# One polynomial moved from GpSimd to VectorE, and a changed start, last group and ending of a mixture-of-experts stage (hybrid decoder trunk, one core)

## The chip, the cores and the metric

The kernel runs on one core of a Trainium2 chip. The metric is the time of one execution on the device in microseconds, as the median of several executions. TensorE (PE in the rows) does the matrix products; PEld is its loading of stationary operands. VectorE is DVE, ScalarE is ACT, GpSimd is POOL, and SP is the engine whose queue issues most transfers.

## What is computed

The input is 1024 tokens of width 1024. The trunk has one layer, so only the Mamba-2 mixer runs, then the expert mixture, the per-layer embedding and a final norm:

```python
h = x
h = h + ssd_mixer(rms_norm(h, ssd_norm), ...)      # dt = softplus(dt_raw + dt_bias), used by the scan
h = h + hier_moe(rms_norm(h, moe_norm), ...)       # 8 groups x 8 experts, top-1 group, top-2 experts in it
gate = sigmoid(rms_norm(h, ple_norm) @ ple_w_gate + ple_b_gate)
h = h + gate * (p @ ple_w_proj)
return rms_norm(h, final_norm)
```

Each of the 64 experts is silu(x @ w_gate) * (x @ w_up) @ w_down with 1024 x 512 weights, so the expert weights are 402.7 MB in fp32 and every one is read once.

## The kernel before

**Mixer (`ssd`).** The tokens are worked in two halves of 512. In each half the input projection runs through four groups of ten column tiles, every product as three fp32r matmuls (high x high, low x high, high x low, L220 to L222), which need each weight split on ScalarE and VectorE (`split`, L70 and L71). Beside it the scan of the group before runs in pieces that a small plan places. `step_sizes` (L225) computes softplus: exp on ScalarE, then s = e/(e+2), q = s*s, and an eight-term polynomial in q by Horner's rule. VectorE computes the first term (L258); seven rounds of a product and a sum are done on GpSimd (L260, L261); VectorE multiplies the result by s (L262). `norm` (L436) makes the row norms of a scan unit on VectorE through `rsqrt` (lines 57 to 67, tiles `nt` and `rs`), and `store` (L444) transposes them on TensorE (L447).

**Order.** Where the text below says that TensorE's order is written by hand, `manual_schedule` fixes it. The order on the other engines is made by a planner ahead of time, from program order and from estimated times. On the chip each engine then takes its instructions in that order.

**Loading of experts.** The unit is a slab of 1 MB ([128, 2048] fp32). `moe_weights.loads` (L840) is a generator that is stepped once per step of the output projection: the gate weights `wpg` of the embedding, the norms, and then the first nine slabs, seven into the ring's buffers (`RING = 7`) and two into `self.spare`, the pair buffers in which later tokens of the groups are gathered. `moe` then loads three more into `ring2`, `yx` and `vx` (L1009). From there `half` (L861) loads each slab into the next of eight buffers, seven of `ring` and one of `ring2`; the load waits in SP's queue until TensorE is through with the buffer's old slab.

**Groups.** For each of the eight groups, `steps` is a list of pieces of the expert products: `up` (gate and up products of two experts side by side, two pieces each) and `down`. One piece is 16 records of L1098 on two slabs. `fill` puts other work behind a numbered step, in TensorE's hand-written order. From the second group on it holds the embedding of the group before (`ple`, L939): statistics and transposes (L972, `tr`), eight `gate` pieces of two fp32 matmuls each (L980; each is two records), and two `add` pieces. Before the last group there are two such sets, for the group's rows and for the overflow rows; each has 12 pieces, at the steps listed in L1334. `wk`, `ps1`, `ps2` are small pools; `sts`, `S` hold selection matrices. `fetch_p` (L926) gathers the projected embedding rows into `p0` and `po` on GpSimd's queue.

**Ending.** The last group's last two down products and its own embedding are done together by `ending` (L1179) in four column quarters q. `product(q)` is the down product (slabs from `columns`), `turn(q)` combines the quarter into the rows and transposes it, `gate(q, j)` is the gate product in three fp32r passes (`parts`, L932), and `halves(q)` splits the gate weights of the quarter into high and low parts, on ScalarE (L1239) and GpSimd (L1240), into one buffer that all quarters use in turn. `add(j)` (L1250) applies the sigmoid, multiplies, adds, squares, and lets GpSimd multiply by the final norm's weights (L1262). Two engines then scale by the norm, and GpSimd's queue issues the indirect store (L1281). `combine(3, 1)` (L1283, L1204) finishes the overflow rows.

Of the kernel before, what the change touches and what calls it, by code (L numbers as in the profile page):

```python
# [42 lines left out]
class K:  # L43
# [64 lines left out]
    def ssd(self, left, right):  # L108
# [116 lines left out]
        def step_sizes(hf):  # L225
# [604 lines left out]
    def moe_weights(self, st):  # L830
# [9 lines left out]
        def loads():  # L840
# [12 lines left out]
            self.first = first = [(s_, k0, e + b) for e, s_ in ((0, wg), (0, wu), (2, wg)) for k0 in (0, 4) for b in range(2)]  # L853
            for i, (src, k0, e) in enumerate(first[:RING + 2]):
                w = self.spare[i - RING].rearrange("p i d -> p (i d)") if i >= RING else None
                self.ready.append(self.half(src, e, k0, 4, w))
                yield

        return loads()

    def half(self, src, e, k0, n, w=None):  # L861
# [3 lines left out]
        if w is None:  # L865
            self.turn = (self.turn + 1) % (RING + 1)
            w = (self.ring2 if self.done and self.turn == 0 else self.ring).tile([128, 2048], F32, name="w")
# [4 lines left out]
    def columns(self, src, e, cs):  # L872

        self.turn = (self.turn + 1) % (RING + 1)
        w = (self.ring if self.turn else self.ring2).tile([128, 2048], F32, name="w")
# [5 lines left out]
    def moe_buffers(self, st, ring):  # L881
# [4 lines left out]
        self.p0, self.po = (hp.tile([128, D], F32, name=f"p{i}") for i in range(2))  # L886
        self.iall = hp.tile([128, NGR + NSET], I32, name="iall")
        for x in (self.h0[0], self.ho[0], self.p0, self.po):
            nc.gpsimd.memset(x, 0.0)
# [49 lines left out]
    def ple(self, h, pr, store, wk, pq_, pc_, own=()):  # L939
# [27 lines left out]
        def tr(k0):  # L967
            if k0 == 0:
# [4 lines left out]
            nc.scalar.activation(V["vT"][:, k0:k0 + 4], pt, AF.Copy)  # L973

        def gate(hf, k0):
# [3 lines left out]
            for k in (k0, k0 + 1):  # L979
                nc.tensor.matmul(V["pq"], lhsT=V["vT"][:, k], rhs=wpg[:, k, cs], start=(k == 0), stop=(k == KD - 1))  # L980
# [19 lines left out]
    def moe(self, s2, ring, sa):  # L1000
# [8 lines left out]
        for n, w in enumerate((self.ring2.tile([128, 2048], F32, name="w"), y0, vx)):  # L1009
            src, k0, e = self.first[RING + 2 + n]  # L1010
            self.ready.append(self.half(src, e, k0, 4, w))
# [161 lines left out]
        def ple_of(G, i, own=part):  # L1173
# [3 lines left out]
                bounds_check=T - 1, oob_is_err=False), wk, ps1, ps2, own)  # L1177

        def ending(G):  # L1179
# [52 lines left out]
            def halves(q):  # L1232
                if q == 0:
                    B["w"] = gp.tile([128, 2, 2, 2, 512], F32R, name="XT")
# [285 lines left out]
```

## Time and profile before

| what | value |
|---|---|
| median of 3 executions | 1903.54 us (1902.07 to 1907.86) |
| the profiled execution's own time | 1900.96 us |
| its span in the profile | 1899.0 us |
| TensorE busy | 1823.4 us, 96% |
| VectorE, ScalarE, GpSimd busy | 1032.4, 754.1 and 192.6 us |
| moved by DMA | 548.23 MB |

The span runs from the first to the last record of the execution; 2 us of its time lie outside it. In rows of instructions the first number is the start or the busy time, as each group says; a bracket at the end gives the idle time of the engine just before, and what ended it.

### The profile page before, as it was taken

What the parts mean: (1) busy time and instruction counts of PE and PEld (TensorE: products, weight loads), DVE (VectorE), ACT (ScalarE), POOL (GpSimd) and SP (SyncE); (2) the same over time, 40 slices, a digit from 0 to 9 for tenths busy, and PEclk for the clock granted to TensorE, in tenths of its full rate; (3) what the DMA queues carried; (4) which work ended last, traced back from release to release, by engine and by line L of the source; (5) the groups of instructions that cost most, each with busy time, mean ns of one, the idle gap of its engine ahead of it and who ended that gap; (6) DMA issues with size and microseconds to landing.
All of it is one profiled execution on the core that took longest, in us unless ns stands there. A gap on an engine that the chain in (4) does not pass through costs nothing. (4 is left out here: it accounts for less than half of the span.)

```text
span 1899.0 us, 23199 instructions
## 1 busy us (share of the span) xinstructions
PE 1823.4 (96%) x8692; PEld 1039.2 (55%) x8692; DVE 1032.4 (54%) x2195; ACT 754.1 (40%) x1044; POOL 192.6 (10%) x276
## 2 busy tenths in 40 slices
PE   6999999999999999999999999999999999999996
PEld 3877877778787778873443343433433334334334
DVE  4588889868988866574341433423415243243223
ACT  5577767567776533332121222211212222122223
POOL 0210122202210131012000000000000000000014
PEclk9999999999999999999999999999999999999998
DMA  9343545345334686958999999999999999999993
GB/s 312 97 115 102 141 114 142 92 121 136 107 87 114 209 320 208 349 190 332 423 421 417 404 421 406 418 421 400 422 413 408 421 411 417 421 402 421 344 346 103
DMA packets 195543, 548.23 MB, mean 289 GB/s; under 512 B 16480, under 2 KB 129376, under 8 KB 147296
## 3 DMA queue, kind: packets, MB, share of 16 engines
q1 hardware_dynamic: 179296, 519.32, 73.1%
q10 hardware_dynamic: 11872, 14.51, 2.2%
q0 software_dynamic: 4256, 12.85, 1.8%
q8 instruction: 70, 1.15, 0.3%
q14 instruction: 49, 0.40, 0.1%
HBM read 527.37 MB, written 21.89 MB: 289 GB/s over the span
## 5 line engine op out<-in xcount | busy, mean ns | idle before, releaser
L220 PE MATMUL mm<-xh,wh 128*128 128x512 f32 x640 | 264.7, 414 | 1.3 <-ACT wh L70 1.3
L222 PE MATMUL mm<-xh,wl 128*128 128x512 f32 x640 | 252.4, 394 | 4.1 <-DVE wl L71 4.1
L221 PE MATMUL mm<-xl,wh 128*128 128x512 f32 x640 | 251.2, 393 | 0.0
L1098 PE MATMUL pup<-w,XT 128*64 128x512 f32 x1016 | 243.6, 598 | 3.6 <-DMA w<-in_w_up_dram 3.6
L1098 PE MATMUL pgate<-w,XT 128*64 128x512 f32 x1000 | 231.8, 598 | 0.0
L1098 PE MATMUL py<-w,hT 128*64 128x512 f32 (+1 forms) x1024 | 226.0, 584 | 2.1 <-DMA w<-in_w_down_dram 2.1
L71 DVE TENSOR_TENSOR yx<-py,yx 128x512 fp32r<-128x512 f32 (+1 forms) x68 | 44.8, 659 | 215.7 <-ACT yx L70 215.7
L1098 PEld LDWEIGHTS pup<-w,XT 128*64 128x64 f32 x1016 | 77.8, 136 | 139.6 <-issue 120.3
L1098 PEld LDWEIGHTS py<-w,hT 128*64 128x64 f32 x1024 | 70.8, 136 | 143.7 <-issue 134.4
L1098 PEld LDWEIGHTS pgate<-w,XT 128*64 128x64 f32 x1000 | 68.5, 136 | 134.0 <-issue 131.5
L222 PEld LDWEIGHTS mm<-xh,wl 128*128 128x128 f32 x640 | 120.8, 189 | 32.9 <-DVE wl L71 7.0
L220 PEld LDWEIGHTS mm<-xh,wh 128*128 128x128 f32 x640 | 121.1, 189 | 31.5 <-issue 4.6
L221 PEld LDWEIGHTS mm<-xl,wh 128*128 128x128 f32 x640 | 121.4, 190 | 29.4 <-issue 5.7
L980 PE MATMUL pq<-wpg,vx 128*128 128x512 f32 x256 | 123.2, 607 | 0.0
L71 DVE TENSOR_TENSOR wl<-w,wh 128x1024 fp32r<-128x1024 f32 x80 | 97.9, 1223 | 39.6 <-ACT wh L70 39.5
L1129 ACT ACTIVATE hT<-pt 128x512 f32<-128x512 f32 x31 | 18.4, 595 | 241.0 <-PE pt L1127 241.0
L70 ACT ACTIVATE wh<-w 128x1024 fp32r<-128x1024 f32 x80 | 84.3, 1053 | 74.1 <-PE mm L221 62.7
L333 DVE SCALAR_TENSOR_TENSOR xbc<-raw,convw,xbc 128x512 f32<-128x512 f32 x144 | 107.5, 749 | 3.2 <-ACT xbc L331 2.4
L70 ACT ACTIVATE yx<-py 128x512 fp32r<-128x512 f32 (+1 forms) x68 | 38.9, 572 | 159.4 <-PE py L1098 159.4
L567 PE MATMUL mm<-wl,yh 128*128 128x512 f32 x256 | 98.7, 395 | 2.4 <-DVE wl L578 2.4
L568 PE MATMUL mm<-wh,yl 128*128 128x512 f32 x256 | 97.3, 392 | 0.0
L566 PE MATMUL mm<-wh,yh 128*128 128x512 f32 x256 | 96.2, 401 | 0.7 <-ACT yh L70 0.7
(354 smaller groups left out, 2789.7 us busy)
## 6 DMA issues: line engine op xcount, KB each, us to landing
w<-in_w_up_dram SPq DMA_DIRECT2D x127, 1024.0 KB, 8.9
w<-in_w_gate_dram SPq DMA_DIRECT2D x125, 1024.0 KB, 9.7
w<-in_w_down_dram SPq DMA_DIRECT2D x120, 1024.0 KB, 11.0
w<-in_w_in_dram SPq DMA_DIRECT2D x32, 1024.0 KB, 5.4
w<-in_w_out_dram SPq DMA_DIRECT2D x48, 512.0 KB, 4.9
ac<-acd SPq DMA_DIRECT2D x32, 512.0 KB, 8.8
w<-in_w_in_dram SPq DMA_DIRECT2D x16, 512.0 KB, 5.3
yn<-yz SPq DMA_DIRECT2D x32, 256.0 KB, 3.6
```

Of the source, the lines that this page charges most:

```text
L70: self.nc.scalar.activation(dst_h, src, AF.Copy)
L71: self.nc.vector.tensor_sub(dst_l, src, r_(dst_h))
L220: nc.tensor.matmul(ps, lhsT=wh[:, k], rhs=x[0][:, k], start=(k == 0), stop=False)
L221: nc.tensor.matmul(ps, lhsT=wh[:, k], rhs=x[1][:, k], start=False, stop=False)
L222: mm = nc.tensor.matmul(ps, lhsT=wl[:, k], rhs=x[0][:, k], start=False, stop=(k == KD - 1))
L333: nc.vector.scalar_tensor_tensor(o, raw[:, j:j + HT], convw[:, m, j:j + 1], o, op0=OP.mult, op1=OP.add)
L566: nc.tensor.matmul(po[i][hf], lhsT=yh[:, ts], rhs=wh[:, cs], start=(k == 0), stop=False)
L567: nc.tensor.matmul(po[i][hf], lhsT=yh[:, ts], rhs=wl[:, cs], start=False, stop=False)
L568: nc.tensor.matmul(po[i][hf], lhsT=yl[:, ts], rhs=wh[:, cs], start=False, stop=(k == 15))
L980: nc.tensor.matmul(V["pq"], lhsT=V["vT"][:, k], rhs=wpg[:, k, cs], start=(k == 0), stop=(k == KD - 1))
L1098: nc.tensor.matmul(ps[64 * b:64 * b + 64], lhsT=xt(k0 + k, b), rhs=w[b][:, k, cs], start=(k0 + k == 0), stop=(k0 + k == K - 1))
L1129: nc.scalar.activation(hT, pt, AF.Copy)
```

## The change

- The polynomial of `step_sizes` is done on VectorE with one fused instruction per round, eight in place of GpSimd's fourteen and the closing product.
- A thirteenth slab (half of the first down weights) is loaded ahead, into `p0` and `po`, which become one buffer `pp` on `self.spare`; their memsets go.
- In the last group the two embeddings of the group before take their gates from two parts: the weights are split on ScalarE and VectorE into `rw` (in `ring2`'s buffer, which the ring gives up for this group: `kept`), the rows are split too, and each product is three fp32r matmuls in place of an fp32 one. The pieces are spread over all 20 steps. The gather into `po` moves to the last step.
- In the ending, the split of the last quarter goes into buffers of its own and onto VectorE, ahead of the third quarter's turn; the final norm's product goes to VectorE; `combine(3, 1)` is held until the last scaling has been issued.

```diff
-            nc.vector.tensor_scalar(e, q, 2.0 / 17, 2.0 / 15, op0=OP.mult, op1=OP.add)
-            for n in (13, 11, 9, 7, 5, 3, 1):
-                nc.gpsimd.tensor_mul(e, e, q)
-                nc.gpsimd.tensor_scalar(e, e, 1.0, 2.0 / n, op0=OP.mult, op1=OP.add)
-            nc.vector.tensor_mul(e, e, s)
+            nc.vector.tensor_scalar(e, q, 2.0 / 17, None, op0=OP.mult)
+            for n in (15, 13, 11, 9, 7, 5, 3):
+                nc.vector.scalar_tensor_tensor(e, e, 2.0 / n, q, op0=OP.add, op1=OP.mult)
+            nc.vector.scalar_tensor_tensor(e, e, 2.0, s, op0=OP.add, op1=OP.mult)
...
-            for i, (src, k0, e) in enumerate(first[:RING + 2]):
+            self.first = first = [(s_, k0, e + b, 4) for e, s_ in ((0, wg), (0, wu), (2, wg)) for k0 in (0, 4)
+                                  for b in range(2)] + [(wd, 0, 0, 2)]
+            for i, (src, k0, e, n) in enumerate(first[:RING + 3]):
...
+    def slab(self):
+        self.turn = (self.turn + 1) % (RING + 1)
+        own = self.done and self.turn == 0 and not self.kept
+        return (self.ring2 if own else self.ring).tile([128, 2048], F32, name="w")
...
-        self.p0, self.po = (hp.tile([128, D], F32, name=f"p{i}") for i in range(2))
+        pp = hp.tile([128, 2, D], F32, name="pp")
+        self.p0, self.po = (pp[:, i] for i in range(2))
+        self.spare.append(pp)
...
+            if two:
+                self.split(*(x[:, k0:k0 + 4] for x in V["v"]), pt)
+            else:
+                nc.scalar.activation(V["vT"][:, k0:k0 + 4], pt, AF.Copy)
...
             for k in (k0, k0 + 1):
+                if two:
+                    w = [rw[:, k % 2, x] for x in range(2)]
+                    self.split(*w, wpg[:, k, cs])
+                    self.parts(V["pq"], V["v"], k, w)
+                    continue
...
+                if q == 3:
+                    B["w"].append([x.tile([128, 2, 2, 512], F32R, name="w") for x in (self.ring2, self.ring)])
...
-                        nc.gpsimd.tensor_sub(wl, src, r_(wh))
+                        (nc.vector if q == 3 else nc.gpsimd).tensor_sub(wl, src, r_(wh))
...
-                nc.gpsimd.tensor_mul(o[:, cs], h[:, cs], fn[:, cs])
...
-                        halves(q + 1)
+                        for n in ((1,), (2, 3), ())[q]:
+                            halves(n)
...
+                nc.vector.tensor_mul(o[:, 0:512], h[:, 0:512], fn[:, 0:512])
                 rstd(B["f"], 3)
...
-                nc.vector.tensor_scalar(o[:, 512:], o[:, 512:], r, None, op0=OP.mult)
+                done = nc.vector.scalar_tensor_tensor(o[:, 512:], h[:, 512:], r, fn[:, 512:], op0=OP.mult, op1=OP.mult)
...
-                combine(3, 1)
+                with tc.issue_after(done.ins):
+                    combine(3, 1)
...
+                if prev and not nxt:
+                    self.kept = True
+                    rw = self.ring2.tile([128, 2, 2, 512], F32R, name="w")
+                    at = (2, 2, 3, 4, 5, 6, 6, 7, 8, 9, 10, 10), (11, 11, 12, 13, 14, 15, 15, 16, 17, 18, 19, 19)
+                    for i in range(2):
+                        for n, piece in zip(at[i], ple_of(prev, i, late=(two, rw))):
+                            fill.setdefault(n, []).append(piece)
...
-                    if n == 15:
+                    if n == (15 if nxt else len(steps) - 1):
                         self.fetch_p(g)
```

## Rows read from the trace of the kernel before

**Rows 1.** The page: busy time by engine, and DMA's busy tenths in 40 slices.

```profile
PE 1823.4 (96%) x8692; PEld 1039.2 (55%) x8692; DVE 1032.4 (54%) x2195; ACT 754.1 (40%) x1044; POOL 192.6 (10%) x276
...
DMA  9343545345334686958999999999999999999993
```

**Rows 2.** Busy time by stretch: length, PE, PEld, DVE, ACT, POOL, PEclk, DMA share, GB/s.

```profile
1600.00:1650.00 50.00, 50.00 (x208) 18.19 (x204) 10.41 (x24) 9.34 (x16) 0.00 (x0) 1.00 1.01 421
...
1750.00:1800.00 50.00, 49.68 (x188) 17.93 (x184) 14.74 (x37) 9.18 (x18) 1.02 (x1) 1.00 0.93 360
1800.00:1850.00 50.00, 48.68 (x204) 17.44 (x202) 13.22 (x26) 12.92 (x20) 4.74 (x4) 1.00 0.93 339
1850.00:1900.00 50.00, 31.42 (x232) 23.10 (x226) 18.08 (x52) 18.69 (x43) 21.89 (x19) 0.86 0.34 109
```

**Rows 3.** Waits in 310 to 400 us: total us, times, longest.

```profile
DVE de L262 <- POOL de L261: 4.4, 1, 4.4
...
PE tp L447 <- DVE rs L67: 3.8, 1, 3.8
```

**Rows 4.** Groups on POOL, 334.3 to 343 us (busy, mean ns, idle).

```profile
L260 POOL TENSOR_TENSOR de<-de,dq 128x128 f32<-128x128 f32 x7 | 4.2, 604 | 1.7 <-DVE nt L65 1.2
L261 POOL TENSOR_SCALAR de<-de 128x128 f32<-128x128 f32 x7 | 2.5, 364 | 0.6
```

**Rows 5.** Timeline of DVE, 334.3 to 345 us (start, us, what).

```profile
342.71 0.29 DVE L262 TENSOR_TENSOR de<-de,ds 128x128 f32<-128x128 f32 x1 [4.42 <-POOL de L261]
...
343.86 0.15 DVE L67 SCALAR_TENSOR_TENSOR rs<-nt,nt 128x4 f32<-128x4 f32 x1
```

**Rows 6.** Busy time by stretch around that wait.

```profile
340.00:344.00 4.00, 0.40 (x2) 0.00 (x0) 1.29 (x6) 1.06 (x1) 2.25 (x6) 0.94 0.22 25
344.00:347.00 3.00, 2.84 (x12) 2.22 (x14) 3.00 (x8) 1.93 (x3) 0.19 (x1) 0.51 0.00 0
```

**Rows 7.** Busy time by stretch, between the last early slab and the first group.

```profile
820.00:830.00 10.00, 9.93 (x53) 7.84 (x52) 7.38 (x11) 2.41 (x4) 0.84 (x2) 1.00 0.30 100
```

**Rows 8.** Waits in the first group, 865 to 985 us.

```profile
PEld py L1098 <- DMA w<-in_w_down_dram: 3.9, 2, 2.2
```

**Rows 9.** Timeline of PE: two gate pieces, last group, and a fp32r gate, ending.

```profile
1771.60 3.70 PE L980 MATMUL pq<-wpg,vx 128*128 128x512 f32 x8
...
1775.23 3.65 PE L1098 MATMUL py<-w,hT 128*64 128x512 f32 x16
...
1858.67 0.50 PE L935 MATMUL pq<-XT,ST 128*128 128x512 f32 x1
...
1860.17 0.28 PE L935 MATMUL pgate<-XT,ST 128*128 128x256 f32 x1
```

**Rows 10.** Groups, 1840 to 1899 us and 900 to 1850 us: split and SBUF-only products.

```profile
L1240 POOL TENSOR_TENSOR XT<-wpg,XT 128x512 fp32r<-128x512 f32 x16 | 20.0, 1281 | 29.4 <-ACT XT L1239 29.4
L1239 ACT ACTIVATE XT<-wpg 128x512 fp32r<-128x512 f32 x16 | 9.7, 627 | 8.1 <-PE pup L1098 4.9 <-PE pq L937 1.7 <-PE pup L937 1.3
...
L990 DVE TENSOR_TENSOR ha<-ha,vx 128x512 f32<-128x512 f32 x8 | 5.5, 689 | 0.2
```

**Rows 11.** Timeline at the start of the ending.

```profile
1848.13 0.66 PE L1127 MATMUL pt<-ident,hh 128*128 128x128 f32 x4 [1.32 <-DVE hh L1120]
```

**Rows 12.** Timeline of the last microseconds.

```profile
1881.30 1.11 DVE L63 SCALAR_TENSOR_TENSOR n<-n,n 128x1 f32<-128x1 f32 x1
...
1882.64 0.22 DVE L63 SCALAR_TENSOR_TENSOR n<-n,n 128x1 f32<-128x1 f32 x1
...
1885.06 0.41 DVE L1204 TENSOR_TENSOR hb<-hb,pc 128x256 f32<-128x256 f32 x1
...
1887.09 3.26 POOL L1262 TENSOR_TENSOR hb<-hb,fn 128x512 f32<-128x512 f32 x3 [4.69 <-DVE hb L1260]
...
1887.26 0.42 DVE L1259 TENSOR_TENSOR vx<-vx,hb 128x256 f32<-128x256 f32 x1
1887.71 1.37 DVE L1260 TENSOR_TENSOR hb<-hb,vx 128x256 f32<-128x256 f32 x1
```

More of the change, by code (lines that the diff above doesn't have):

```diff
@@ L865, in half @@
         if w is None:
-            self.turn = (self.turn + 1) % (RING + 1)
-            w = (self.ring2 if self.done and self.turn == 0 else self.ring).tile([128, 2048], F32, name="w")
+            w = self.slab()
         w3 = w.rearrange("p (k f) -> p k f", k=n)
@@ L872, in columns @@
     def columns(self, src, e, cs):
-        self.turn = (self.turn + 1) % (RING + 1)
-        w = (self.ring if self.turn else self.ring2).tile([128, 2048], F32, name="w")
+        w = self.slab()
         w4 = w.rearrange("p (b k c) -> p b k c", b=2, k=4)
@@ L885, in moe_buffers @@
         self.h0, self.ho = ([hp.tile([128, D], F32, name=f"ha{i}"), b[:, 0], b[:, 1]] for i, b in enumerate(self.spare))
[L886 removed]
+        pp = hp.tile([128, 2, D], F32, name="pp")
+        self.p0, self.po = (pp[:, i] for i in range(2))
+        self.spare.append(pp)
         self.iall = hp.tile([128, NGR + NSET], I32, name="iall")
[L888 removed]
+        for x in (self.h0[0], self.ho[0]):
             nc.gpsimd.memset(x, 0.0)
@@ L937, in parts, with ple @@
         mm(to, lhsT=v[1][:, k], rhs=w[0], start=False, stop=(k == KD - 1))
-    def ple(self, h, pr, store, wk, pq_, pc_, own=()):
+    def ple(self, h, pr, store, wk, pq_, pc_, own=(), two=None, rw=None):
         nc = self.nc
@@ L967, in tr @@
         def tr(k0):
-            if k0 == 0:
+            if k0 == 0 and two:
+                V["v"] = two()
+            elif k0 == 0:
                 new("vT", [128, KD, 128])
@@ L1009, in moe @@
         for n, w in enumerate((self.ring2.tile([128, 2048], F32, name="w"), y0, vx)):
-            src, k0, e = self.first[RING + 2 + n]
-            self.ready.append(self.half(src, e, k0, 4, w))
+            src, k0, e, m = self.first[RING + 3 + n]
+            self.ready.append(self.half(src, e, k0, m, w))
         self.done, self.turn = True, 0
@@ L1171, in two, with ple_of @@
                     (sts[0].rearrange("p i j t -> p i (j t)"), g0.tile([128, 2, 512], F32R, name="S"))]
-        def ple_of(G, i, own=part):
+        def ple_of(G, i, own=part, late=()):
             n = NGR + SET[G.g] if i else G.g
@@ L1176, in ple_of @@
                 out=self.out, out_offset=self.rows(n), in_=v, in_offset=None,
-                bounds_check=T - 1, oob_is_err=False), wk, ps1, ps2, own)
+                bounds_check=T - 1, oob_is_err=False), wk, ps1, ps2, own, *late)
         def ending(G):
@@ L1400, in all @@
         sa.close()
-        self.ready, self.done, self.turn = [], False, 0
+        self.ready, self.done, self.kept, self.turn = [], False, False, 0
         def after():
```

14 lines of the change are left out of this document (7 added, 7 removed).

## The prediction, made before the changed kernel was run

> **What bounds the kernel now.** I read the page's shares first: TensorE is busy 96% of the span [rows 1], so an edit counts only where TensorE waits, where it does fewer records, or after its last one. The second half of the slices shows DMA at 9 tenths throughout [rows 1], so I asked by stretch which of the two is late. In the middle of the expert stage DMA's share is 1.01 at 421 GB/s [rows 2]: a slab of 1.049 MB takes 2.49 us, and TensorE follows the transfers, though closely. In the last group the share falls to 0.93 and 360 and 339 GB/s while TensorE is busy 49.68 and 48.68 of 50 us [rows 2]: buffers are full, and TensorE sets the pace. In the last 50 us it is busy 31.42 [rows 2], the rest being the chain that closes the kernel. Then the waits of each changed place.
>
> **The polynomial.** In the second half VectorE stands idle 4.4 us for GpSimd's polynomial, and TensorE 3.8 us for the row norms `rs` [rows 3]. These are one event: VectorE's L262 waits for GpSimd until 342.71, and the last step of `rs`, which has nothing to do with the polynomial, stands behind it and ends at 344.01 [rows 5]. GpSimd's fourteen instructions are 4.2 + 2.5 = 6.7 us with 2.3 us of gaps [rows 4]. The new chain is eight fused instructions and a first product; taking L262's 0.29 us for each [rows 5], eight make 2.3 us where L262 was 0.29. VectorE had 4.42 us free there, so even if all of them stand ahead of `rs`, it ends 4.42 - 2.0 = 2.4 us earlier; if the planner puts `rs` first, the 3.8 us vanish. With the wait goes a clock drop: after it TensorE was granted 0.51 for 3 us, its lower level of 1.2 GHz, with 2.84 us of work [rows 6], about 1.4 us more than at 2.4 GHz. I take -3.5 us. Ends: -5.2 (3.8 + 1.4) and 0, if TensorE meets the next late instruction of a full VectorE. The first half's GpSimd chain I cost at nothing: that wait has no counterpart on TensorE among the waits I read.
>
> **One more slab ahead.** Between the early loads and the first group DMA is nearly free (0.30, 100 GB/s) [rows 7], so a slab into `pp` costs nothing there, wherever SP's queue issues it between the output weights' loads and the three late slabs; nothing waits for those stores of `ppd` soon. Afterwards every load is one slab further. The first group waits 3.9 us for down weights [rows 8], more than the 2.49 us won, and DMA is saturated from there to the last group [rows 2], so the whole lead is kept: -2.5 us. It can't be more; it is 0 if TensorE turns out the tighter of the two in the groups between. The memsets that go were on an idle GpSimd.
>
> **The last group's gates.** Sixteen pieces of two fp32 products. Two pieces, eight records, go from 1771.60 to 1775.23, 3.63 us; two products in three fp32r records each go from 1858.67 to 1860.17, 1.50 us [rows 9]. Old: 16 x 1.815 = 29.0 us. New: 16 x 1.50 = 24.0, and with a switch of 0.2 us back to the experts' records after each, since pieces no longer stand in pairs, 27.2. I take 25.6, 3.4 us less. One piece now stands behind the last step, where TensorE waited 1.32 us for VectorE's `hh` [rows 11]; that hides 1.3 more. So -4.7 on TensorE. Against it: 32 weight splits, each 0.63 us on ScalarE and about 0.69 on VectorE [rows 10], 20 and 22 us beside a load of 9 to 13 and 13 to 15 us per 50 [rows 2]. There is room, and nearly a whole step (3.65 us, a block of L1098 in [rows 9]) between a piece and the next, in which two splits take some 2.2 us; but `rw` holds just one piece's weights, so a split can't start before the piece ahead is through. I charge 0.7 us of waits: -4.0. Ends: -6.3 (without any switch) and +1. Transposed rows, now split as well, add 0.69 us of VectorE to four transposes, with a step to spare. With seven buffers a step's two slabs need 4.98 us of DMA and TensorE at least 3.6 + 1.5 = 5.1 us, so DMA stays just ahead.
>
> **The move past the ending's start.** The second `add` now falls after step 19. Its table load, sigmoid, squares and norm on ScalarE and VectorE stand among the first products' splits, and on GpSimd's queue the `po` gather waits for this `add`, with the first quarter's splits and the store behind or around it. The nearest row is the 0.69 us of an addition [rows 10]; I charge one such delay, +0.6 (0 to +2).
>
> **The ending.** While GpSimd works, one step of the row norm takes 1.11 us where the same step later takes 0.22 [rows 12]: 0.9 us on the path. L1204 takes 0.41 us of VectorE in the final chain at 1885.06, of which 0.35 delays the next product; it moves behind the last scaling and there is covered by the output's transfer. The last addition takes 1.37 us beside GpSimd's L1262, against 0.42 for a product of that size [rows 12]: 0.95 us. The final product on VectorE (0.69 us by [rows 10]) lies beside the last square and costs some 0.1, the fused scaling another 0.1. So -2.0 us (-1.2 to -2.3). The last quarter's split moved ahead: ScalarE's eight copies in a row may delay the third quarter, +0.4.
>
> Of this pairing the rows show that VectorE instructions with both inputs in SBUF stretch while GpSimd runs. The Trainium skill, SBUF — State Buffer, section "SBUF: two separate sides", says the two share a port pair under an exclusive lock, the loser waiting for the whole instruction. That speaks against the fourth quarter's subtractions on VectorE beside the third's on GpSimd. The trace agrees as far as 1.11 against 0.22 us goes [rows 12]; by the rule the sum below would be -8.0 in place of -11.0, the case that the rival "port" works out from rows.
>
> **Sum.** -3.5 - 2.5 - 4.0 + 0.6 - 2.0 + 0.4 = -11.0 us. Against the profiled execution's 1900.96 (span 1899.0 and 1.96 around it) that is 1890.0; the median is 2.58 above it, so 1892.5.
>
> **The rivals.**
> *Splits too slow for their single buffer*: the gates' gain of 4.7 us is paid back in small waits of 0.3 us at each of 16 pieces: 1892.5 + 4.0 = 1896.5. For: ScalarE also changes tables in this group. Against: free time by the stretches. Chance 0.15.
> *The wait at 340 us only moves*: VectorE is busy 3.00 of 3 us right behind it [rows 6], so the next norm or split is late: 1896.0. Chance 0.10.
> *Port*: in the ending four subtractions of 0.69 us each wait behind a GpSimd one of 1.28 [rows 10], 5.1 us more on VectorE, of which the quarters' own slack should cover some 2: +3, 1895.5. Chance 0.06. The third quarter's split on GpSimd is then late too.
> *Slower: splits queued behind their own customers.* If the planner places ScalarE's copies of a piece behind the `Silu` or `hT` copy of the step before it, which wait for that step on TensorE, each piece exposes a copy and a subtraction of both halves, 2 x 0.63 + 2 x 0.69 = 2.6 us less the first half's overlap, say 1.5. Sixteen make +24 in place of the 0.7 charged: 1892.5 + 23.3 = 1916. It decides from 11.7 / 16 = 0.73 us a piece, where it is level with before; so half of its chance goes to "same". Against: the planner puts ready work first, and a copy is ready a step early. Chance 0.05.
> Two of the first three together give about 1900: chance 0.04. My forecast: 0.60.
>
> **How the numbers follow.** The range reaches from the best ends of the two largest terms (-5.2 and -6.3 for -3.5 and -4.0, 1888.5, and 2 us for the median's own spread) to two rivals together: 1886.5 to 1900.0. About 0.3%, 5.7 us, is what a measurement of this kernel can tell from no change. Faster means under 1897.8: the forecast and most of the first three rivals, 0.82. Same: the pairs (0.04), a quarter of the first three (0.075) and half of the slower case (0.025), 0.14. Slower: its other half and 0.015 for what none of these names, 0.04.
>
> **What would show it.** TensorE's wait for `rs` near 340 us gone or under 1.6 us, and no lowered clock after it. DMA still at 1.0 to the last group, which starts some 6 us earlier. L980 groups in the last group replaced by L935-to-L937 form, with no wait over 0.5 us for their parts; the time from the group's start to the ending 4 us shorter. In the last chain no 1.11 and 1.37 us steps. A group of waits of TensorE for split weights of more than 5 us, or for DMA in the last group, would prove me wrong there; a gain from the polynomial under 1 us would name the moved wait.

## The result, and the profile after

The changed kernel takes 1891.16 us (median of five executions, 1889.39 to 1895.57) where the kernel before takes 1903.54: ratio 0.9946, 95% interval 0.9930 to 0.9963, so 7 to 13 us faster and outside the 0.3% that a measurement can tell from nothing. The prediction was 1892.5 us, its range 1886.5 to 1900.0. The two profiled executions have spans of 1899.0 and 1889.4 us, 9.6 us apart.

Lines of the changed kernel, for reading its rows: polynomial L260 and L261, store transposes L446, output projection L565 to L567, `parts` L942 to L944, an fp32 gate product L998, expert products L1116, hh transposes L1145, the ending's combination L1220 and L1222, its splits L1260 and L1261, its last additions L1280 and L1281, the final norm's product L1298.

The page of the changed kernel: busy time by engine, and DMA's tenths ([rows 1] before).

```profile
PE 1818.2 (96%) x8724; PEld 1045.4 (55%) x8724; DVE 1058.4 (56%) x2250; ACT 767.5 (41%) x1072; POOL 163.2 (9%) x239
...
DMA  9344535444434686958999999999999999999992
```

Busy time by stretch of the changed kernel: length, PE, PEld, DVE, ACT, POOL, PEclk, DMA share, GB/s ([rows 2, 6] before).

```profile
1600.00:1650.00 50.00, 50.00 (x209) 18.11 (x209) 11.81 (x25) 10.12 (x17) 0.00 (x0) 1.00 1.01 421
1750.00:1800.00 50.00, 49.98 (x221) 21.90 (x222) 25.61 (x50) 21.14 (x37) 1.02 (x1) 1.00 1.00 401
1800.00:1850.00 50.00, 48.38 (x245) 22.94 (x245) 26.72 (x53) 23.48 (x42) 6.02 (x5) 1.00 1.03 371
...
340.00:344.00 4.00, 4.00 (x41) 3.07 (x40) 4.00 (x11) 3.26 (x5) 0.62 (x1) 1.00 0.09 29
344.00:347.00 3.00, 3.00 (x16) 2.40 (x15) 3.00 (x6) 0.35 (x1) 1.79 (x3) 1.00 0.30 96
```

At 340 to 347 us TensorE is busy throughout at the full clock, where it stood for 3.6 us and then had 0.51 [rows 6]. In the last group DMA's share is 1.00 and 1.03 in place of 0.93, so DMA now keeps pace with a faster TensorE without holding it up: 49.98 of 50 us are busy. ScalarE and VectorE carry 11 to 14 us more in each of the two stretches, for the most part the splits.

The timeline of the changed kernel, VectorE and TensorE, around `rs`; then TensorE's first product of the last group, its first gate piece and the start of the ending; then VectorE and GpSimd at the end ([rows 5, 9, 11, 12] before).

```profile
339.50 0.15 DVE L67 SCALAR_TENSOR_TENSOR rs<-nt,nt 128x4 f32<-128x4 f32 x1
...
340.35 0.60 PE L446 MATMUL tp<-ident,rs 128*128 128x128 f32 x4
...
1732.30 3.65 PE L1116 MATMUL pgate<-w,XT 128*64 128x512 f32 x16
...
1749.91 0.50 PE L942 MATMUL pq<-w,ST 128*128 128x512 f32 x1
...
1751.50 3.65 PE L1116 MATMUL pgate<-w,XT 128*64 128x512 f32 x16
...
1838.77 0.60 PE L1145 MATMUL pt<-ident,hh 128*128 128x128 f32 x4
...
1843.66 0.78 PE L1220 MATMUL pc<-yx,ST 128*128 128x256 f32 x2 [0.38 <-ACT yx L70]
1845.05 0.38 PE L1220 MATMUL pc<-yx,ST 128*128 128x256 f32 x1 [0.61 <-DVE yx L71]
1846.05 0.44 PE L1239 MATMUL pt<-ident,hb 128*128 128x128 f32 x2 [0.62 <-DVE n L57]
...
1877.88 0.42 DVE L1280 TENSOR_TENSOR vx<-vx,hb 128x256 f32<-128x256 f32 x1
1878.22 0.68 DVE L1298 TENSOR_TENSOR hb<-hb,fn 128x512 f32<-128x512 f32 x1
...
1878.82 0.42 DVE L1281 TENSOR_TENSOR hb<-hb,vx 128x256 f32<-128x256 f32 x1
...
1882.04 0.75 DVE L1302 SCALAR_TENSOR_TENSOR hb<-hb,ss,fn 128x512 f32<-128x512 f32 x1
1882.70 0.41 DVE L1222 TENSOR_TENSOR hb<-hb,pc 128x256 f32<-128x256 f32 x1
1883.59 0.99 POOL L1303 DMA_INDIRECT out_dram<-hb,iall  x1 [17.85 <-DVE hb L1222]
```

`rs` is ready before its transposes, which no longer wait. A gate piece takes 1.59 us from its start to the next block (1749.91 to 1751.50). The hh transposes start without a wait. Three waits stand at the start of the ending, 1.61 us in sum, where the kernel before has two, 0.17 and 0.51 us. At the end the stretched addition is 0.42 us (1.37 in [rows 12]), but the final product L1298 stands ahead of it. The row of the store names L1222, but GpSimd's own wait for it lasts 19.72 us from 1863.11, to 1882.83: L1302 is through then (1882.04 and 0.75), L1222 is not.

By the start times of the same TensorE records in both executions (milestones), the 9.6 us come together thus: the first expert product starts 2.0 us earlier (864.42 against 866.38), the last group 3.1 (1732.30 against 1735.39) and the hh transposes 9.4, so 6.3 more inside the group; the ending's start gives 1.2 back, the last chain takes 1.7 off, and the store starts 0.25 later behind its scaling. How far such differences repeat is the next section's first question.

### The profile page after: what moved, and what is told of

It reads as the page before. It is cut to its first block, busy times and chain, and to the rows that moved or that the text cites. A ratio compares the mean times of both kernels' runs of the same rounds, so it can differ in the third digit from the quotient of the medians.

```text
span 1889.4 us, 23328 instructions
## 1 busy us (share of the span) xinstructions
PE 1818.2 (96%) x8724; PEld 1045.4 (55%) x8724; DVE 1058.4 (56%) x2250; ACT 767.5 (41%) x1072; POOL 163.2 (9%) x239
## 4 chain that ended last, share of the span: by engine, by line
PE 74%; DVE 10%; DMA 10%; ACT 3%; issue 3%; POOL 0%; SPq 0%; ACTq 0%; POOLq 0%; DVEq 0%
PE pgate L1116 11%; PE pup L1116 10%; PE py L1116 9%; PE mm L222 5%; PE mm L221 5%; PE mm L220 5%; PE pq L998 5%; PE pc L1106 4%; DMA w<-in_w_up_dram 4%; PE mm L567 2%; PE mm L566 2%; PE mm L565 2%; DMA ac<-acd 2%; PE pc L1179 2%; PE py L413 1%
## 5 line engine op out<-in xcount | busy, mean ns | idle before, releaser
L1116 PE MATMUL pup<-w,XT 128*64 128x512 f32 x1016 | 242.6, 598 | 3.4 <-DMA w<-in_w_up_dram 3.4
L1116 PE MATMUL pgate<-w,XT 128*64 128x512 f32 x1000 | 232.0, 599 | 0.0
L1116 PE MATMUL py<-w,hT 128*64 128x512 f32 (+1 forms) x1016 | 225.9, 583 | 2.5 <-DMA w<-in_w_down_dram 2.5
L1116 PEld LDWEIGHTS pup<-w,XT 128*64 128x64 f32 x1016 | 78.6, 136 | 136.3 <-issue 116.9
L1116 PEld LDWEIGHTS py<-w,hT 128*64 128x64 f32 x1016 | 69.9, 136 | 140.6 <-issue 132.8
L1116 PEld LDWEIGHTS pgate<-w,XT 128*64 128x64 f32 x1000 | 68.6, 136 | 134.6 <-issue 132.5
L567 PE MATMUL mm<-wh,yl 128*128 128x512 f32 x256 | 97.3, 392 | 1.8 <-DVE yl L71 1.8
L565 PE MATMUL mm<-wh,yh 128*128 128x512 f32 x256 | 96.2, 401 | 1.3 <-ACT yh L70 0.9
L998 PE MATMUL pq<-wpg,vx 128*128 128x512 f32 x192 | 93.4, 609 | 0.0
## 6 DMA issues: line engine op xcount, KB each, us to landing
w<-in_w_down_dram SPq DMA_DIRECT2D x119, 1024.0 KB, 10.2
```

What stands on the lines that cost most here:

```text
L565: nc.tensor.matmul(po[i][hf], lhsT=yh[:, ts], rhs=wh[:, cs], start=(k == 0), stop=False)
L567: nc.tensor.matmul(po[i][hf], lhsT=yl[:, ts], rhs=wh[:, cs], start=False, stop=(k == 15))
L1116: nc.tensor.matmul(ps[64 * b:64 * b + 64], lhsT=xt(k0 + k, b), rhs=w[b][:, k, cs], start=(k0 + k == 0), stop=(k0 + k == K - 1))
```

## The experiments

All are edits of the changed kernel and ran against the kernel before.

| kernel | median, us | ratio to before (95%) |
|---|---|---|
| changed again (e0) | 1893.29 | 0.9951 (0.9935 to 0.9966) |
| polynomial on GpSimd (e1) | 1896.20 | 0.9965 (0.9953 to 0.9976) |
| no 13th slab (e2) | 1895.49 | 0.9960 (0.9945 to 0.9975) |
| old gates (e3) | 1899.75 | 0.9983 (0.9972 to 0.9995) |
| old ending (e4) | 1892.03 | 0.9948 (0.9934 to 0.9963) |
| five y buffers (e5) | 1892.21 | 0.9943 (0.9927 to 0.9959) |
| gates in pairs (e6) | 1893.48 | 0.9950 (0.9933 to 0.9968) |
| fp32 gates, spread (e7) | 1898.74 | 0.9974 (0.9962 to 0.9987) |
| one step earlier (e8) | 1899.36 | 0.9974 (0.9962 to 0.9986) |
| earlier, and turned (e9) | 1898.09 | 0.9970 (0.9959 to 0.9982) |
| first split on VectorE (e11) | 1891.32 | 0.9940 (0.9920 to 0.9960) |
| e11 and e5 (e12) | 1890.68 | 0.9936 (0.9915 to 0.9956) |

Intervals of 4 to 8 us don't resolve steps of 1 or 2, so the steps are read from start times within each profile.

**e0: the changed kernel again.** No edit.

> The changed kernel once more, unedited, beside the others of this call: what one execution's steps repeat. Theory (the differences read so far between profiled executions are those of the edits where they exceed about 1 us): span 1888 to 1891 us, milestones within 1 us of the first profile after the first 200 us are taken off; whether the clock falls at the start of the ending, near 1841 us, as it did in two of the four kernels with the new gates or their like, is open. Rival (executions of one kernel differ by 2 us and more, so that the terms can't be read from single profiles): 2 us or more at one of the milestones.

Span 1889.0 us, but by another way. From the transposes at 265 us to those at 340 us the two executions agree within 0.02 us; counted from there, at the first expert product this one is 3.6 us ahead, at the last group's start 0.5. The rival holds from 600 us to the last group: a difference of some 3 us between two profiles proves nothing there. Inside the last group the two agree again: 106.46 and 106.47 us from its first product to the hh transposes. So I read the steps only in stretches that repeat.

**e1: the polynomial back on GpSimd.**

```diff
-            nc.vector.tensor_scalar(e, q, 2.0 / 17, None, op0=OP.mult)
-            for n in (15, 13, 11, 9, 7, 5, 3):
-                nc.vector.scalar_tensor_tensor(e, e, 2.0 / n, q, op0=OP.add, op1=OP.mult)
-            nc.vector.scalar_tensor_tensor(e, e, 2.0, s, op0=OP.add, op1=OP.mult)
+            nc.vector.tensor_scalar(e, q, 2.0 / 17, 2.0 / 15, op0=OP.mult, op1=OP.add)
+            for n in (13, 11, 9, 7, 5, 3, 1):
+                nc.gpsimd.tensor_mul(e, e, q)
+                nc.gpsimd.tensor_scalar(e, e, 1.0, 2.0 / n, op0=OP.mult, op1=OP.add)
+            nc.vector.tensor_mul(e, e, s)
```

> The changed kernel with the polynomial back on GpSimd; all else as changed. Theory (the wait for rs near 340 us was worth 4.7 us at 420 us, but 2.8 us of it were given back at 642 to 656 us, where ScalarE stands for the transfer of y): TensorE is 4.3 to 4.7 us behind the changed kernel between 420 and 610 us, only 1.5 to 2.5 us behind at the first expert product, and the span is 1.5 to 2.5 us longer, 1891 to 1892 us against 1889.4. Rival (the 3.5 us of the prediction, the loss at 650 us having another cause, such as the other edits' new order of loads): 3.5 us or more behind at the first expert product and at the end, 1893 us or more. Rival 2 (the polynomial is worth nothing, the planner having merely reordered): under 1 us everywhere.

Waits of e1 from 310 to 400 us (total us, times, longest):

```profile
DVE de L262 <- POOL de L261: 4.4, 1, 4.4
...
PE tp L447 <- DVE rs L67: 3.8, 1, 3.8
```

Both waits of [rows 3] are back, to the tenth. From 265 to 340 us the kernels with the polynomial on GpSimd take 78.31 (before) and 78.32 us (e1), the twelve others 74.82 to 74.85: 3.5 us for the wait alone. Only those two show the clock lowered to 0.5 behind it, for 3.4 us at 343.5 and 344.1 us. From the transposes at 265 us to those at 420 us, where this counts too, the kernel before takes 157.7 us and the ten with the new polynomial that share its other lowered clock, near 403 us, 152.8 to 153.7: 4.0 to 5.0 us in all. The first-half chain cost nothing in either form: between 194 and 266 us the kernel before and the changed one drift apart by 0.04 us. The expected 4.3 to 4.7 us between 420 and 610 us weren't there (2.2 at 420 us, or 3.1 when the 0.9 us by which e1 is early at 265 us are counted in; e1 has no lowered clock near 403 us). A worth of 1.5 to 2.5 us at the end is not settled by this run (2.0 us behind at the first expert product, 4.5 in the span, 1.6 of it a lowered clock in the ending); e5 takes it up.

**e5: five buffers for y.**

```diff
-                y = wp.tile([128, 384], F32, name="y", bufs=3)
+                y = wp.tile([128, 384], F32, name="y", bufs=5)
```

> The changed kernel with five buffers for y in the output projection in place of three; only the places of the y loads in ScalarE's queue move, two loads earlier. Theory (the polynomial's gain is given back at 640 to 656 us because ScalarE, in order, stands for y's transfer, and the scan's exponentials and VectorE's low part of y stand behind it): ScalarE's waits for y shrink from 9.9 us to under 4, and 2 to 2.8 us are kept from 656 us to the end, span 1886.6 to 1887.4 us. Rival (the loads wait for the scan's own stores of yn, or the scan's chain is what is late, so that earlier loads land no earlier): under 0.7 us, the waits for y as before. Rival 2 (the time is kept up to the first expert product and lost there to the transfers of the slabs, which don't start earlier): 2 us or more ahead at 700 us, under 1 us at 930 us.

ScalarE's waits from 640 to 660 us, kernel before, changed kernel (with one wait of TensorE from 636 to 665 us below), e5 (there the longest wait, none for y):

```profile
ACT yh L70 <- DMA y<-yn: 5.2, 1, 5.2
```

```profile
ACT yh L70 <- DMA y<-yn: 9.9, 3, 6.1
...
PE mm L567 <- DVE yl L71: 1.8, 1, 1.8
```

```profile
ACT yh L70 <- PE mm L566: 4.3, 3, 2.7
```

The loads of y stand in ScalarE's own order, and a copy that waits for one holds up the scan's exponentials behind it, then VectorE's L396 and the low part of y. From the store transposes at 623 us to those at 678 us the kernel before and e1 take 52.0 and 52.1 us. Of the ten profiles with the new polynomial and three buffers, two take 52.0 and 52.1; seven take 53.4 to 54.7 and one 56.0, with a lowered clock in the stretch; in these eight TensorE waits 0.7 to 2.0 us for VectorE's low part of y. With five buffers (e5, e12) it is 51.9 both times and neither wait is there. So 1.4 to 2.7 us are usually lost here to y's transfer, and two more buffers keep them. That it is the polynomial's gain that is given back fits these times but isn't shown: the old polynomial has two profiles only, and two of the ten with the new one show no loss either, though their code up to here is that of the other eight. In the medians (e5 against e0 -1.1 us, e12 against e11 -0.6) this is within the intervals, and e5's own profile lost as much at 607 us to a clock lowered for 10.2 us, so the expected span of 1887 us was missed (1888.2).

**e2: no thirteenth slab.**

```diff
-                                  for b in range(2)] + [(wd, 0, 0, 2)]
+                                  for b in range(2)]
...
-            for i, (src, k0, e, n) in enumerate(first[:RING + 3]):
+            for i, (src, k0, e, n) in enumerate(first[:RING + 2]):
...
-            src, k0, e, m = self.first[RING + 3 + n]
+            src, k0, e, m = self.first[RING + 2 + n]
```

The memsets of `p0` and `po` are back as well.

> The changed kernel with twelve slabs ahead, as before the change; all else as changed. Theory (the slab is worth what the first groups kept, 1.2 to 1.6 us, because the transfer was not what every wait of the first group was for): level with the changed kernel at the first expert product, 1.2 to 1.6 us behind it from 930 us on and at the end, span 1890.6 to 1891.0 us. Rival (the 2.5 us of the prediction, one transfer's time, hidden in the difference of the two kernels by another loss): 2.2 to 2.8 us behind. Rival 2 (worth nothing, the 1.6 us came from the other edits): under 0.6 us.

The stretch 890 to 930 us, columns as above, in the kernel before, the changed kernel and e2:

```profile
890.00:930.00 40.00, 39.39 (x181) 14.47 (x179) 12.56 (x23) 4.78 (x8) 0.99 (x1) 1.00 0.98 401
```

```profile
890.00:930.00 40.00, 40.00 (x184) 14.69 (x184) 13.55 (x25) 4.78 (x8) 1.61 (x2) 1.00 1.01 411
```

```profile
890.00:930.00 40.00, 39.47 (x181) 13.97 (x179) 12.85 (x26) 4.78 (x8) 0.99 (x1) 1.00 0.97 398
```

TensorE's waits for weights from 865 to 985 us, the window of [rows 8], changed kernel, then e2:

```profile
PEld py L1116 <- DMA w<-in_w_down_dram: 4.2, 2, 2.5
...
PEld pup L1116 <- DMA w<-in_w_up_dram: 0.6, 1, 0.6
```

```profile
PEld py L1116 <- DMA w<-in_w_down_dram: 4.3, 3, 2.4
...
PEld pup L1116 <- DMA w<-in_w_up_dram: 2.0, 2, 1.4
```

The wait for down weights, 3.9 us before, is shortened in no profile (3.9 to 4.5 us in the twelve with the slab). What shrinks is the wait for up weights: 2.1 us in the kernel before and 2.0 in e2, 0.6 to 1.9 in the twelve.

From the first expert product to hh transposes some 200 us later, e2 takes 203.3 us and the kernel before 203.2, the changed kernel 202.0; all twelve profiles with the slab lie between 201.7 and 203.1. So the slab is ahead there by 0.1 to 1.6 us. In the rows TensorE waits 0.5 to 0.6 us in this stretch with twelve slabs, and DMA isn't full: 13 GB/s less over 40 us is 0.52 MB, half a slab, or 1.2 us at 421 GB/s. I read this as the reason why it isn't 2.5; no run tests it. And the lead isn't seen to last: from the first expert product to the last group's start both profiles without the slab take 869.0 us, the twelve with it 867.1 to 872.6.

**e3: the old gates at their old steps.**

```diff
-                if prev and not nxt:
...
-                elif prev:
+                if prev:
...
-                    if n == (15 if nxt else len(steps) - 1):
+                    if n == 15:
```

> The changed kernel with the last group's two embeddings in fp32 and at their old steps, and the gather of po at step 15; polynomial, slab and ending as changed. Theory (the gates from parts took 6.4 us out of the last group and put 1.3 us in at the start of the ending): level up to the last group's start, 6.4 us behind at the end of its last step, 5.1 us behind from the second product of the ending on, span 1894.5 us. Rival (part of the 6.4 us belongs to the better supply by the other edits, and shows in this kernel too): 4 us or less behind. Rival 2 (the 1.3 us at the ending's start come from the ending's own new order, so they stay): 6 us or more behind at the end.

**e7: fp32 gates at the new steps.**

```diff
-                    rw = self.ring2.tile([128, 2, 2, 512], F32R, name="w")
...
-                        for n, piece in zip(at[i], ple_of(prev, i, late=(two, rw))):
+                        for n, piece in zip(at[i], ple_of(prev, i, late=())):
```

> The changed kernel with the last group's gates as fp32 products again, but at the changed kernel's steps (spread over 20, the gather of po at the last); rw and the splits go. Theory (the arithmetic of the prediction: 16 pieces at 1.82 us in fp32 against 1.5 to 1.6 from parts, and a piece at the last step hides the wait for hh in either form): the last group is 3.5 to 5.2 us longer than in the changed kernel, with no wait for hh at its end, and 1.2 us at the ending's start stay as they are. Rival (the parts cost more in switches than the records show, and the spread alone gave the 6.4 us): under 2 us. Rival 2 (most of the 6.4 us is the parts): 6 us or more.

TensorE's timeline of e3, then of e7, where the last group starts and ends:

```profile
1732.47 3.65 PE L1116 MATMUL pgate<-w,XT 128*64 128x512 f32 x16
...
1845.19 0.65 PE L1145 MATMUL pt<-ident,hh 128*128 128x128 f32 x4 [1.29 <-DVE hh L1138]
```

```profile
1736.78 3.65 PE L1116 MATMUL pgate<-w,XT 128*64 128x512 f32 x16
...
1846.38 1.98 PE L998 MATMUL pq<-wpg,vx 128*128 128x512 f32 x4
1848.20 0.60 PE L1145 MATMUL pt<-ident,hh 128*128 128x128 f32 x4
```

From the last group's first product to the hh transposes: e3 112.72 us, e7 111.42, changed kernel 106.47, and all eight profiles with the changed gates and steps 106.45 to 106.47. So the spread is worth 1.30 us, the wait for hh that the last piece now covers, and the parts are worth 4.95: 0.31 a piece. Summed from each record's start to the next one's, the sixteen pieces take 29.1 us in the kernel before and in e3, 29.8 in e7 and 25.1 in the changed kernel. The theory held in both; the gate pieces carry more of the gain than I had predicted, and they are the largest part of the change (the medians of e3 and e7 are 6.5 and 5.5 us above that of e0).

**e6: the first embedding's pieces in pairs.**

```diff
-                    at = (2, 2, 3, 4, 5, 6, 6, 7, 8, 9, 10, 10), (11, 11, 12, 13, 14, 15, 15, 16, 17, 18, 19, 19)
+                    at = (2, 2, 3, 3, 4, 4, 6, 7, 7, 8, 8, 10), (11, 11, 12, 13, 14, 15, 15, 16, 17, 18, 19, 19)
```

> The changed kernel with the first embedding's eight gate pieces of the last group in pairs behind four steps (3, 4, 7, 8) in place of one behind each of eight steps; the second embedding and all else as changed. Rival of the prediction (the splits are too slow for the single buffer rw as soon as two pieces stand together): TensorE waits for the second piece's weights 1 to 2.6 us at each of four pairs, 4 to 10 us in the last group. Theory (a half of rw is free as soon as its product is through, so that only a part of a copy and a subtraction, 0.63 and 0.69 us a product, shows): 0.5 to 1.3 us a pair, 2 to 5 us in all. Rival 2 (no wait at all, the spread over 20 steps was not needed for the buffer): under 0.5 us in all.

TensorE's timeline of e6, the second piece of the first pair:

```profile
1751.91 0.50 PE L942 MATMUL pq<-w,ST 128*128 128x512 f32 x1
1752.63 0.50 PE L943 MATMUL pq<-w,ST 128*128 128x512 f32 x1 [0.22 <-DVE w L71]
```

2.25 us longer (108.72 against 106.47), 0.56 a pair: the theory, at its lower end. The single buffer does bind, but only when a piece follows another at once. One step of expert products (3.65 us) between them hides the splits fully, and that is why the changed kernel shows no wait for parts.

**e8: the second embedding one step earlier.**

```diff
-                    at = (2, 2, 3, 4, 5, 6, 6, 7, 8, 9, 10, 10), (11, 11, 12, 13, 14, 15, 15, 16, 17, 18, 19, 19)
+                    at = (2, 2, 3, 4, 5, 6, 6, 7, 8, 9, 9, 10), (10, 10, 11, 12, 13, 14, 14, 15, 16, 17, 18, 18)
```

> The changed kernel with the second embedding of the last group one step earlier, its last gate and addition behind step 18 in place of 19 (two pieces more stand in pairs). Theory (the 1.2 us at the ending's start come from the embedding's last addition among the first product's splits, and the 1.3 us of TensorE's wait for hh are covered only by the gate piece at step 19): the waits for yx and n at the ending's start go, about 1.2 us, and the wait for hh of 1.3 us ahead of the pt transposes is back: level, within 0.5 us of the changed kernel, at the ending's second product. Rival (the pieces in pairs wait for the single buffer rw as well): 1 us or more behind. Rival 2 (only one of the two waits matters): 1 us or more ahead.

VectorE's and GpSimd's timeline of e8 beside the ending's first splits:

```profile
1845.42 1.10 DVE L1138 SCALAR_TENSOR_TENSOR hh<-sg,gw,pup 128x512 f32<-128x512 f32 x1
...
1847.02 0.15 DVE L60 TENSOR_SCALAR n<-n 128x1 int32<-128x1 int32 x1
1847.21 0.95 DVE L63 SCALAR_TENSOR_TENSOR n<-n,n 128x1 f32<-128x1 f32 x1
1848.19 1.20 DVE L67 SCALAR_TENSOR_TENSOR n<-n,n 128x1 f32<-128x1 f32 x1
1849.43 1.20 DVE L63 SCALAR_TENSOR_TENSOR n<-n,n 128x1 f32<-128x1 f32 x1
1850.66 1.19 DVE L67 SCALAR_TENSOR_TENSOR n<-n,n 128x1 f32<-128x1 f32 x1
...
1846.87 4.97 POOL L1261 TENSOR_TENSOR XT<-wpg,XT 128x512 fp32r<-128x512 f32 x4 [0.47 <-ACT XT L1260]
```

My theory fell: not level, but 2.6 us longer to the hh transposes and 1.4 from there to the second product. The planner put the last addition ahead of `hh`, which is through at 1846.52, and TensorE waits 2.07 us for it; one pair of pieces more adds some 0.5 (0.56 a pair in e6). The row norm then runs exactly beside GpSimd's four subtractions: four steps of 0.95 to 1.20 us where each takes 0.16 to 0.22 alone, 3.8 us more of VectorE. For 2.31 us TensorE stands for a low part `yx` behind them. The step with one tensor operand that falls beside them (L60, 0.15) isn't stretched.

**e9: e8, with the hh transposes behind the ending's first product.**

```diff
+                    if q == 0 and j == 1:
+                        turned()
...
-                    flush()
-                    ending(cur)
+                    ending(cur, flush)
```

> The kernel of e8_one_step_earlier, and the pt transposes of the last hh stand behind the ending's first product, that of the experts before (1.95 us that need no hh), in place of ahead of it. Theory: the wait for hh is covered by that product, and the ending starts without either wait: 1.2 to 1.4 us ahead of the changed kernel at the ending's second product and at the end, no lowered clock near 1841 us. Rival (the second product of the ending waits for hT, which now comes later): the gain is under 0.4 us.

The rival: the second product waits 1.90 us for hT, since the first covers most of the wait for `hh` (0.35 us are left) but not the copy behind it. The clock was lowered there after all, for 3.4 us at 1846.8 and again at 1853.6. From the last group's start to the ending's first `pt` it takes 117.5 us, e8 117.7 and the changed kernel 113.8.

**e11: the first quarter's split on VectorE.**

```diff
-                        (nc.vector if q == 3 else nc.gpsimd).tensor_sub(wl, src, r_(wh))
+                        (nc.vector if q in (0, 3) else nc.gpsimd).tensor_sub(wl, src, r_(wh))
```

> The changed kernel with the ending's first quarter split on VectorE in place of GpSimd (four subtractions); all else as changed. Theory (VectorE's instructions with both inputs in SBUF stretch beside GpSimd's splits; L1007, 1.61 us beside them where L1008 takes 0.74, holds up the low parts yx and with them the ending's first combination): L1007 takes 0.7 us, the three waits at the ending's start (0.38, 0.61 and 0.62 us on yx, yx and n) shrink by 0.7 us or more in sum, and the end comes 0.7 to 1.2 us earlier, up to 2.8 where the changed kernel's execution had a clock drop behind these waits. Rival (the four subtractions, 2.8 us more on VectorE, hold up the same chain by as much): within 0.4 us. Rival 2: 1 us or more later.

VectorE and GpSimd at the ending's start in the changed kernel, then VectorE in e11:

```profile
1842.06 1.61 DVE L1007 TENSOR_TENSOR vx<-vx,pp 128x512 f32<-128x512 f32 x1 [2.34 <-ACT vx L1002]
...
1838.13 5.00 POOL L1261 TENSOR_TENSOR XT<-wpg,XT 128x512 fp32r<-128x512 f32 x4 [38.70 <-ACT XT L1260]
```

```profile
1841.17 0.69 DVE L1007 TENSOR_TENSOR vx<-vx,pp 128x512 f32<-128x512 f32 x1 [0.42 <-ACT vx L1002]
```

L1007 falls from 1.61 to 0.69 us as expected, but TensorE's way from the hh transposes to the ending's first `pt` only from 7.29 to 6.89 us (6.10 in e3, without a late addition). The three waits are still 1.50 us in sum (1.61 in the changed kernel). That is the first rival's size, 0.4 us, and not the 0.7 expected. So moving the splits off GpSimd takes a third of the 1.2 us away, net of the four subtractions that VectorE gets in their place. The rest no run took away; the table load, the sigmoid and the addition among the first product's splits are what stands there, but that they are the cause isn't shown.

**e4: the old ending.** The functions `halves`, `add` and `finish` as before the change, `combine(3, 1)` not held back.

> The changed kernel with the ending as before the change (splits of all quarters on GpSimd into one buffer, the final norm's product on GpSimd, the overflow rows' last combination not held back). Theory (the ending's edits are worth 1.7 us behind the last gate product and nothing ahead of it, less 0.2 us at the store): level up to the last gate product's start, 1.5 us behind at the store, span 1890.9 us; one step of the row norm at 1.1 us and the last addition at 1.4 us are back. Rival (the split on VectorE pays for the third quarter too, and GpSimd's old split of the last quarter would be late behind the faster last group): 3 us or more, with a wait of TensorE for XT. Rival 2 (the tail only moved to the store): under 0.5 us.

VectorE and GpSimd of e4 in the last chain:

```profile
1872.12 1.12 DVE L63 SCALAR_TENSOR_TENSOR n<-n,n 128x1 f32<-128x1 f32 x1
...
1877.59 2.25 POOL L1280 TENSOR_TENSOR hb<-hb,fn 128x512 f32<-128x512 f32 x2 [4.37 <-DVE hb L1278]
...
1877.76 1.49 DVE L1277 TENSOR_TENSOR vx<-vx,hb 128x256 f32<-128x256 f32 x1
1879.17 0.41 DVE L1222 TENSOR_TENSOR hb<-hb,pc 128x256 f32<-128x256 f32 x1
1879.51 0.61 DVE L1278 TENSOR_TENSOR hb<-hb,vx 128x256 f32<-128x256 f32 x1
```

From the start of the last gate record to the end of the span: 15.83 us in e4, 14.18 in the changed kernel, 1.65 us. As expected, the step of the row norm is back (1.12 us beside GpSimd's splits of the last quarter, 0.22 in the changed kernel), and so are the stretched product (1.49 against 0.42) and the combination ahead of the addition; up to the last gate the two agree within 0.1 us, so the last quarter's split on VectorE neither costs nor pays on TensorE. The medians don't show the 1.65 us (0.9948 for e4, 0.9946 and 0.9951 for the changed kernel).

**e12: e11 and e5 together.**

> The kernel of e11_first_split_dve with the five y buffers of e5_y_bufs. If both hold what they are meant to: ScalarE's waits for y under 4 us, the ending's start as in e11, 1 to 2 us ahead of the changed kernel in the median. Rival (neither is worth anything that five rounds can show): within 1 us of it.

No wait for y, the ending's start as in e11, and the lowest median of all, 1890.68 us; its lead on the changed kernel (0.5 us, and 2.6 on the repeat e0) is within the intervals: the rival can't be excluded.

## Why the prediction was right, and where its steps were off

The time came out 1.3 us under the number, by the forecast's mechanism and none of the rivals. The terms, though, missed in both directions and cancelled, so that the closeness is in part luck; the repeat's median, 1893.29, lies on the other side of the number. The sum was -11.0 us; the profiled executions differ by 9.6, the medians by 12.4.

- **Polynomial, -3.5.** Right in mechanism, a little small at its place: the wait alone gave 3.5 us, and with the lowered clock, which the term had counted in, it is 4.0 to 5.0. "The wait at 340 us only moves" is refuted there: 3.00 of 3 us busy at the full clock right behind. What I had not looked for is 300 us further on: the output projection, where 1.4 to 2.7 us are usually lost at y's three buffers. If that is the gain given back, the rival named the mechanism (the next late instruction) and the wrong place. By the first expert product single profiles can't tell any more: from the transposes at 265 us the kernel before takes 600.5 us, e1 601.8, the twelve others 595.3 to 603.1.
- **Slab, -2.5.** Its steps failed. The size rested on the 3.9 us of [rows 8], and that wait for down weights stayed (4.2 us in the changed kernel); a shorter one, for up weights, shrank from 2.0 or 2.1 to 0.6 to 1.9 us. "DMA is saturated from there to the last group": [rows 2] show 1.01 for 1600 to 1650 us, and I carried it back to the first group, where the share was 0.98. What came in the first 200 us of the groups is 0.1 to 1.6 us. And "so the whole lead is kept": at the last group's start no run shows any of it, among profiles that spread by 5.5 us in between.
- **Gates, -4.0.** The mis-sized term: -6.3. That is the figure of the range's better end, but not by its way, which took 24.0 us for the new pieces. They take 25.1 in place, 1.48 to 1.59 each, where I had 25.6; the old ones took 29.1, as said (29.0). So the pieces gave 4.0 in place of 3.4, and the hidden wait 1.3, as said. The charge of 0.7 us of waits for `rw` fell away, since there is none. The remaining 1.0 us is in records beside the pieces, at which I had not looked: the products `pc<-yx` of the group take 6.4 us (7.1 before), the transposes of `hh` 1.2 (1.6). "Splits too slow" needs pieces in pairs, as e6 shows.
- **Past the ending's start, +0.6.** 1.2 us, and more in half of the profiles, where a lowered clock follows the waits (below). The step named the late addition; it didn't price GpSimd's first splits beside it (L1007, 1.61 us in place of 0.69).
- **Tail, -2.0 and +0.4.** 1.65 us came in sum by e4, as against 1.6, but again with misses that cancel. The stretched instructions went as said (the norm's step, 0.9 us, and the last addition), and the last quarter's split ahead cost nothing. But the final product, charged 0.1 us beside the last square, stands in VectorE's order ahead of the last addition and costs 0.60 there (1878.22 to 1878.82); behind it, it might lie beside the square, which no run tried.
- **"Port".** The planner put VectorE's subtractions for the fourth quarter between 1844.9 and 1851.8 us, 0.67 to 0.69 us each, when GpSimd's splits of the first quarter were through (1843.1) and those of the second not begun (1852.3). They never met, so the rival's price wasn't paid, and wasn't tested either. Its mechanism is real where they do meet: 1.61 us for L1007, and in e8 about 1.2 us a step beside subtractions of 1.24 us (4.97 / 4). The Trainium skill, SBUF — State Buffer, section "SBUF: two separate sides", says that the loser waits for the whole instruction, and that VectorE joins this lock with two inputs in SBUF; e8 agrees with both, as each stretched step is about as long as one subtraction and L60, with one tensor, isn't stretched. Beside the splits of the second quarter in the changed kernel, L1222, whose second operand `pc` is in PSUM, the memory that TensorE writes, keeps its 0.42 us as well.

The forecast signs: the wait for `rs` gone, no wait for parts, no 1.11 and 1.37 us steps, the last group 6.3 us shorter. Wrong was that it would start 6 us earlier: 3.1 in this pair of executions. The nine profiles whose edits, if any, lie in the last group or behind it spread by 8.7 us at that point, counted from the transposes at 265 us, and the kernel before lies among them, so its true size stays open.

## What to carry to other kernels

Price a replaced piece of work in its place, together with the records beside it, and ask for each piece what stands between it and the next: one step of cover made the single buffer free, none cost 0.56 us a pair. A lead that is won early can be lost again at a later prefetch of fixed depth: look there for a wait that takes it back, and read DMA's share, and ask which transfer a wait is for, in the stretch where the lead is to pay, not in a later one. VectorE chains of small steps with two SBUF inputs shouldn't run beside GpSimd's large ones: taking the last quarter's split off GpSimd gave the norm's 0.9 us back at no cost, while taking the first quarter's off it netted 0.4, since its work then stood in VectorE's own order.

## What the runs showed of the hardware

Small waits can be followed by a lowered clock. In ten profiles whose ending starts with waits of some 1.3 to 1.6 us in sum (the changed gates, or late fp32 ones as in e7), TensorE's granted clock then fell to 0.5, its lower level of 1.2 GHz, for 3.4 us in five, and not in the other five; the changed kernel's first profile is one of those without, its repeat one of those with it. TensorE's timeline of the repeat:

```profile
1843.05 0.38 PE L1220 MATMUL pc<-yx,ST 128*128 128x256 f32 x1 [0.61 <-DVE yx L71]
1844.05 0.44 PE L1239 MATMUL pt<-ident,hb 128*128 128x128 f32 x2 [0.62 <-DVE n L57]
...
1844.89 3.27 PE L1116 MATMUL py<-w,hT 128*64 128x256 f32 x16
```

The sixteen records take 3.27 us where the same ones take 1.95 in the changed kernel's first profile, and the ending is 1.7 us longer. The kernel before and e3, with waits of 0.17 and about 0.5 us there, show no such drop; e8 and e9, with longer waits, both do. So the place for which the prediction took 0.6 us costs 1.2 or 2.9, and nothing in these runs says which it will be. Likewise the lowered clock near 607 us lasted 3.4 us in some executions and 10.2 in another of the same code (e8), and executions of the same code differed by up to 7.7 us at the first expert product, counted from the transposes at 265 us, while inside the last group they agree to 0.02 us.
